# Fifth raw weight tile and two-part bias matmul in the first stage, two recurrence projections beside keys and values in the mixer

## The chip, the cores and the metric

The kernel runs on one core of a Trainium2 chip. The metric is the device time of one execution in microseconds, the median of three runs. TensorE (PE) does the matmuls, VectorE (DVE) and ScalarE (ACT) the elementwise work, GpSimd (POOL) small work and its own DMA queue, SyncE (SP) issues the weight DMAs.

## The reference

A hybrid encoder of two layers on a sequence of 256 positions and 1024 channels, in float32. Every layer is a half-weighted gated feed-forward block, a mixer, and a second feed-forward block, with a final norm behind the last layer:

```python
for l in range(DEPTH):                       # DEPTH = 2
    x = x + 0.5 * swiglu(rms_norm(x, ffn1_norm[l]), ffn1_w_gate[l], ffn1_w_up[l], ffn1_w_down[l])
    h = rms_norm(x, mix_norm[l])
    xr, gate, q, k, v = jnp.split(h @ w_in[l], SPLITS, axis=-1)   # 512, 512, 512, 128, 128 columns
    y_rec = recurrent_group(xr, gate, ...)   # convolution of 4 taps, two gated linear recurrences
    y_att = windowed_gqa(q, k, v, attn_sink[l], rel_bias)         # 8 heads, 2 key heads, window 128
    x = x + concat([rms_norm(y_rec, ...), rms_norm(y_att, ...)]) @ w_out[l]
    x = x + 0.5 * swiglu(rms_norm(x, ffn2_norm[l]), ...)
return rms_norm(x, final_norm)
```

The feed-forward width is 2816. The attention bias is a table of 32 rows per head, looked up by the bucket of the distance.

## The kernel before, in words

All products are of float32 accuracy, made of TensorE's faster format fp32r: a value is split into a high part (a rounding copy) and a low part (the value less the high part), and three products are summed. Weights come from DRAM as raw tiles of 1 MB (`load_raw`, L225 to L249, on SP's queue), a column chunk of 256 columns ("kc") or 256 rows ("rc"). There are RAWS = 3 raw buffers, and raw number 3 goes into another tile ("w") that is free until the first mixer. `prep_one` (L268 to L311) turns a raw tile into halves of 128x1024: ACT makes the high part (L303; for a few names DVE does, L301), DVE the low part (L304). Halves go into a ring of SLOTS = 8 slots; the two of the mixer's keys and values ("kv", 0 and 1) go into the tiles "w" and "i" in its stead. When the last half of a raw tile is made, the next raw tile is loaded into its buffer. Halves are made AHEAD = 3 places ahead of the matmul that uses them.

There are six stages: feed-forward, mixer, feed-forward, twice. PE, SP and POOL run in the order of the program text; on ACT and DVE a planner orders the work by what is ready and, among that, by the text, except in the first steps (FIRST, L53), the last and where a helper says so.

A feed-forward stage takes its 22 units of 128 columns in turn. Units 0 and 1 are done together, positions as stationary operand (`head`, L690, with 512 moving columns; in the first stage `first_head`). The others are done by `gu` (L749), weights as stationary operand: a product for the gate (g2, g3, ...), one for the up projection (u2, u3, ...), each some 2.8 us of PE, then `whole`, `gated` and `split_h` on ACT and DVE. `head_end` (L726) transposes units 0 and 1 behind u2 and splits them. Down products (d0, d1, ...) follow five units later. All gate and up products take their PSUM bank from two pools of two banks in turn (`bank("gc")`).

In the first stage the order of raw tiles is gate and up of units 0/1 (raw 0, 1), of units 2/3 (2, 3), of units 4/5 (4, 5), down of units 0/1 (6), gate of 6/7 (7), and so on. Raw 0 and 1 are split in quarters by `first_prep` (L251; token w11 is the high part of the second quarter of raw 1, on ACT). The stage also fetches parameters: `setup_params` at unit 4 (POOL's queue), the recurrence's gate weights (`load_gates`, L359, a memset and eight DMAs on POOL's queue into tile "i", at unit GLOAD = 4), the mixer's gain (`load_gain(1)`, L1149, SP's queue, before the unit loop) and, at unit 9, `setup_params2` with the bias product of the table (33x8) and a 33x512 one-hot (L458, plain float32).

At the boundary to a mixer (`boundary`, L588) the last down products run (`tail`), the rows are normalized, `transposes(0)` turns the first 128 positions, `head(0)` computes keys and values of these, `transposes(1)` and `head(1)` do the other 128. In the mixer `head` (L846) is 24 matmuls of 256 columns by `natural` (L545). Then the units follow in the list ORDER (L59): x is one of four recurrence inputs (`xr`, L868: 24 matmuls of 256 columns, then the convolution `conv`, L873, four DVE steps that read the PSUM bank), k turns the keys (`head_end`, L861), q queries, l the recurrence's gate products (`lru_gate`, L891: 12 matmuls into two banks, eight ACT steps), L attention logits (`att_logits`, L959: two banks, four DVE steps and four ACT exponentials), g the output gate, P, V, s, c, y, D, O, r, R, S the rest.

Of the kernel before, what the change touches and what calls it, by code (L numbers as in the profile page):

```python
# [8 lines left out]
F32 = mybir.dt.float32  # L9
F32R = mybir.dt.float32r  # L10
# [21 lines left out]
MIXF = 0  # L32
TAIL = 4
HB = 7
GLOAD = 4
GSPLIT = 12
X1 = False
EXTRA = {("kv", 0): "w", ("kv", 1): "i"}
# [17 lines left out]
CUT = 3  # L56
RCUT = 1
EARLY = 1
ORDER = "x0 k0 x1 q0 l0 q1 l1 L0 x2 L1 x3 g0 l2 P0 q2 l3 V0 P1 s0 L2 g1 c0 c1 q3 V1 P2 L3 c2 y0 g2 y1 V2 P3 g3 c3 V3 D0 y2 y3 r0 O0 r1 O1 r2 r3 R0 R1 R2 R3 S0".split()  # L59
HEAD = 2  # L60
VO = 6
VG = 1
# [5 lines left out]
def encoder_kernel(  # L68
# [81 lines left out]
    def cols(w, c):  # L150
        return add_raw(w[:, c:c + 256].rearrange("(k p) c -> p k c", p=128), "kc")
# [7 lines left out]
    def head_half(name, r, j):  # L159
        add_half(name, [(r, j)], "kh")  # L160
# [26 lines left out]
        down(NM // 2 - 1)  # L187

    def plan_mix(st, wi, wo):
        r = cols(wi, 1536)  # L190
        for j in range(2):
            head_half((st, "kv", j), r, j)
        chunk = {}

        def chunk_of(n, p):
            if (n, p) not in chunk:
                chunk[n, p] = cols(wi, {"x": 0, "g": 512, "q": 1024}[n] + p * 256)
            return chunk[n, p]

        for n, i in ORDER:  # L200
            i = int(i)
            if n in "xg":
                col_half((st, {"x": "xr", "g": "gt"}[n], i), chunk_of(n, i // 2), i % 2)
            elif n == "q":
                add_half((st, "q", i), [(chunk_of("q", h), i * 64, h * 64, 64) for h in range(2)], "kc")
        for p in range(4):
            r = rows(wo, p * 256)
            for j in range(2):
                add_half((st, "o", 2 * p + j), [(r, j)], "rc")
# [15 lines left out]
    def load_raw():  # L225
        r = state["raw"]
        if r >= len(raws):
            return
        src, shape = raws[r]
        if r == RAWS:  # L230
            t = w_p.tile([128, 2048], F32, tag="w", name="raw")
        else:
            t = raw_p.tile([128, 2048], F32, tag="raw", name="raw")
        if shape == "kc":
            v = t.rearrange("p (k c) -> p k c", k=KD)
        else:
            v = t.rearrange("p (k c) -> p k c", k=2)
        raw_t[r] = (v, src)
        if r < 2:
            if r == 1:  # L240
                for q in range(4):
                    if q == XQ:
                        load_x(1)
                    for n in range(2):
                        vv, ss = raw_t[n]
                        nc.sync.dma_start(out=vv[:, 2 * q:2 * q + 2, :], in_=ss[:, 2 * q:2 * q + 2, :])
        else:
            nc.sync.dma_start(out=v, in_=src)
        state["raw"] = r + 1  # L249

    def first_prep(lo, n, q):  # L251
        name = ((0, 0), "gu"[n], q // 2)
        if name not in slot_t:
            slot_t[name] = tuple(ring_p.tile([128, 1024], F32R, tag=w, name=w) for w in ("wh", "wl"))
        src = raw_t[n][0][:, 2 * q:2 * q + 2, :]
        c = q % 2 * 512
        h3, l3 = (w[:, c:c + 512].rearrange("p (k c) -> p k c", k=2) for w in slot_t[name])
        if lo:
            dve.tensor_sub(out=l3, in0=src, in1=h3.bitcast(F32))
        else:  # L260
            act.activation(out=h3, in_=src, func=AF.Copy)
        if lo and n and q == 3:
            state["half"] = 4
            for n in range(2):
                del raw_t[n]
                load_raw()

    def prep_one():  # L268
        j = state["half"]
        name, pieces, form = halves[j]  # L270
        for pc in pieces:
            while state["raw"] <= pc[0]:
                load_raw()
        if name in turns:
            wh = ring_p.tile([128, 1024], F32R, tag="wh", name="wh")
            wl = ring_p.tile([128, 1024], F32R, tag="wl", name="wl")
        else:
            n = EXTRA[name[1:]]
            if n == "pr":
                wh, wl = (pr_p.tile([128, 1024], F32R, tag=n, name="w_pr") for _ in range(2))  # L280
            else:
                w = {"w": w_p, "i": mix_p}[n].tile([128, 2048], F32R, tag=n, name="w_" + n)
                wh, wl = w[:, 0:1024], w[:, 1024:2048]
        for pc in pieces:
            v = raw_t[pc[0]][0]
            if form == "kc":
                _, c, d, n = pc
                src = v[:, :, c:c + n]
                h3 = wh.rearrange("p (k c) -> p k c", k=KD)[:, :, d:d + n]
                l3 = wl.rearrange("p (k c) -> p k c", k=KD)[:, :, d:d + n]  # L290
            elif form == "kh":
                src = v[:, 4 * pc[1]:4 * pc[1] + 4, :]
                h3, l3 = (w.rearrange("p (k c) -> p k c", k=4) for w in (wh, wl))
            elif form == "gu":
                src = v[:, 2 * pc[1]:2 * pc[1] + 2, :]
                h3, l3 = (w.rearrange("p (k n c) -> p k n c", k=2, n=2)[:, :, pc[2], :] for w in (wh, wl))
            else:
                src = v[:, pc[1], :]
                h3, l3 = wh, wl
            if name[0][1] == 1 and name[1:] in VHI:  # L300
                dve.tensor_copy(out=h3, in_=src)  # L301
            else:
                act.activation(out=h3, in_=src, func=AF.Copy)  # L303
            dve.tensor_sub(out=l3, in0=src, in1=h3.bitcast(F32))  # L304
        slot_t[name] = (wh, wl)
        state["half"] = j + 1
        for pc in pieces:
            if last_use[pc[0]] == j:
                del raw_t[pc[0]]
                if pc[0] != RAWS:  # L310
                    load_raw()  # L311

    def prefetch(target):
# [122 lines left out]
    def setup_params():  # L436
        tmp = a_p.tile([128, 2, 512], F32, tag="a", name="tmp")
        rows_t = tmp[:N_ROWS, 0, :]
        srcs = [(R_CONVW, conv_w.rearrange("l j c -> (l j) c")), (R_CONVB, conv_b),
                (R_BA, lru_b_a.rearrange("l d c -> (l d) c")), (R_BX, lru_b_x.rearrange("l d c -> (l d) c")),  # L440
                (R_LAM, lru_lambda.rearrange("l d c -> (l d) c")), (R_GREC, lru_out_norm), (R_GATT, attn_out_norm)]
        for r, s in srcs:
            pool.dma_start(out=rows_t[r:r + s.shape[0], :], in_=s)
        pool.dma_start(out=sink_t, in_=attn_sink.partition_broadcast(128))
        rb = mix_p.tile([128, T], F32, tag="k", name="rb")[:33, :NH]
        oh = tmp[:33, 1, :]
        pool.memset(rb[32:33, :], -1e30)
        pool.dma_start(out=rb[0:32, :], in_=rel_bias)
        pool.dma_start(out=oh, in_=onehot)
        return tmp, rows_t, rb, oh  # L450

    def setup_params2(tmp, rows_t, rb, oh):
        ps = bank("gc")
        for c in range(NT):
            pe.transpose(ps[:, c * N_ROWS:(c + 1) * N_ROWS], rows_t[:, c * 128:(c + 1) * 128], eye_t[:N_ROWS, :N_ROWS])
        act.activation(out=par.rearrange("p a b -> p (a b)"), in_=ps[:, :NT * N_ROWS], func=AF.Copy)
        ps = bank("gc")
        pe.matmul(ps[:NH, :], rb, oh, start=True, stop=True)  # L458
        line = tmp[:NH, 0, :]
        act.activation(out=line, in_=ps[:NH, :], func=AF.Copy)  # L460
        ld = dram.tile([NH, 512], F32, name="ld")
# [220 lines left out]
    def ffn(st, acc_done):  # L682
# [112 lines left out]
        def body():  # L795
            nd = 0
            for m in range(HEAD, NM):
# [6 lines left out]
                if m == HEAD:  # L804
                    head_end()
                if st == (0, 0):
                    if m == 4:
                        late_setup.append(setup_params())
                    if m == 9:
                        setup_params2(*late_setup.pop())  # L810
# [16 lines left out]

    def mix(l):
        st = (l, 1)
        ps_x = {}  # L830
        xch_t, xcl_t = {}, {}
        xc_t, ge_t, a_t, yh_t, yl_t = {}, {}, {}, {}, {}
        q_t = mix_p.tile([128, NT, T], F32R, tag="q", name="q_t")
# [10 lines left out]
            return ps  # L844

        def head(t):  # L846
            if t == 0:
                ps_x["kv"] = bank("gc")
            ps = ps_x["kv"]
            natural([ps[:, t * 256:t * 256 + 256]], [[W(st, "kv", j) for j in range(2)]], t)  # L850
            if t == 1:
                for j in range(2):
                    done((st, "kv", j))
                new_tiles()
                act.activation(out=kv_t.rearrange("p t c -> p (t c)"), in_=ps, func=AF.Copy)

        def new_tiles():
            late["w"] = w_p.tile([128, 2 * NT, T], F32, tag="w", name="w_t")
# [7 lines left out]
            dve.tensor_sub(out=kl_t, in0=ps[:, 0:T], in1=k_t.bitcast(F32))  # L866

        def xr(i):  # L868
            ps = unit("xr", i)
            with tc.high_priority(offset=MIXF):  # L870
                conv(i, ps)

# [258 lines left out]
    with tc.manual_schedule(engines={engines.PE, engines.SP, engines.Pool}):  # L1131
# [4 lines left out]
            step[n.upper()] = lambda *a, f=f: f(True, *a)  # L1136
        with tc.manual_schedule(engines={engines.Activation, engines.DVE}):
            setup_early()
            for _ in range(RAWS + 1):
                load_raw()  # L1140
            for tok in FIRST:
                ins = step[tok[0]](*map(int, tok[1:]))
                if tok in BEHIND:
                    state["behind"].append(ins)
# [1 line left out]
        state["behind"] = [ins]  # L1146
        prefetch(3 + LEAD2)
        state["behind"] = []
        load_gain(1)  # L1149
        for s in range(3 * DEPTH):  # L1150
            _, body, tail, evac = stages[s]
            body()
# [54 lines left out]
```

## Time and profile before

| | |
|---|---|
| median of 3 runs | 940.21 us (939.73 to 942.36) |
| the profiled execution, its own time | 940.3 us |
| its span in the trace | 938.5 us |
| PE busy | 925.9 us (99%) |
| DVE busy | 696.5 us (74%) |
| ACT busy | 544.7 us (58%) |
| POOL busy | 37.0 us (4%) |
| granted TensorE clock, mean | 0.999 |

Times in the trace count from the start of the span. The ends of matmuls are modelled, so that a matmul of 256 columns is shown with some 0.28 us although the next starts 0.12 us later: what a matmul costs is read from start to start.

### The profile page before, as it was taken

Reading aid. Unit: us, or ns where it says so; the run is one execution under the profiler, and the core shown is the slowest. Engines: PE = TensorE matmul, PEld = TensorE weight load, DVE = VectorE, ACT = ScalarE, POOL = GpSimd, SP = SyncE. Lnnn points to the kernel's source line nnn. Section 1 sums busy time; section 2 is a strip of 40 time slices with the busy share of each in tenths; the row PEclk is TensorE's granted clock in tenths of the full one; section 3 lists DMA queues with packets and bytes.
Section 4 is the critical chain, followed back from the end, with each engine's and each line's share of the span. In section 5 each row is a group of like instructions: output and inputs, shape, how many; then the busy total and the mean of one; then the engine's idle time right before and its main releaser. Section 6 shows DMA issues by size and latency. Waiting matters only on the chain.

```text
span 938.5 us, 13682 instructions
## 1 busy us (share of the span) xinstructions
PE 925.9 (99%) x5288; PEld 804.8 (86%) x5288; DVE 696.5 (74%) x1212; ACT 544.7 (58%) x1006; POOL 37.0 (4%) x58
## 2 busy tenths in 40 slices
PE   8999999999999999999999999999999999999997
PEld 7888888889988888888888888888999888888885
DVE  6877666759998866666688666666799887666663
ACT  7755555547865655555466555554687565555542
POOL 4100000000010000000030000000000100000000
PEclk9999999999999999999999999999999999999999
DMA  8966955614255866565557565655162566665521
GB/s 279 304 211 200 326 192 183 228 64 154 91 157 179 262 197 191 179 192 196 175 174 252 181 186 198 199 179 179 49 223 68 180 233 203 197 196 182 184 86 45
DMA packets 124993, 172.54 MB, mean 184 GB/s; under 512 B 3920, under 2 KB 108792, under 8 KB 124928
## 3 DMA queue, kind: packets, MB, share of 16 engines
q1 hardware_dynamic: 122192, 166.21, 54.7%
q0 software_dynamic: 2288, 4.87, 1.6%
q8 instruction: 41, 0.67, 0.3%
q10 hardware_dynamic: 448, 0.59, 0.2%
q14 instruction: 24, 0.20, 0.1%
HBM read 170.59 MB, written 3.16 MB: 185 GB/s over the span
## 4 chain that ended last, share of the span: by engine, by line
PE 92%; ACT 2%; DVE 2%; DMA 1%; issue 1%; POOL 0%; POOLq 0%; DVEq 0%; ACTq 0%
PE ps_g L572 16%; PE ps_c L572 15%; PE ps_g L571 7%; PE ps_c L571 7%; PE ps_a L581 5%; PE ps_a L583 4%; PE ps_a L582 4%; PE ps_b L582 4%; PE ps_b L583 4%; PE ps_b L581 4%; PE ps_g L697 2%; PE ps_c L697 2%; PE ps_a L1010 1%; PE ps_g L561 1%; PE ps_g L560 1%; PE ps_g L562 1%
## 5 line engine op out<-in xcount | busy, mean ns | idle before, releaser
L304 DVE TENSOR_TENSOR wl<-raw,wh 128x1024 fp32r<-128x1024 f32 (+1 forms) x320 | 367.4, 1157 | 106.3 <-ACT wh L303 101.9
L303 ACT ACTIVATE wh<-raw 128x1024 fp32r<-128x1024 f32 (+1 forms) x306 | 301.6, 1000 | 89.0 <-PE ps_b L583 61.8
L572 PE MATMUL ps_g<-xhl,wh 128*128 128x512 f32 x640 | 231.5, 396 | 1.5 <-DVE hl L746 1.5
L572 PE MATMUL ps_c<-xhl,wh 128*128 128x512 f32 x640 | 231.2, 396 | 0.0
L571 PE MATMUL ps_g<-xhl,wl 128*128 128x256 f32 x560 | 156.5, 279 | 0.0
L571 PE MATMUL ps_c<-xhl,wl 128*128 128x256 f32 x560 | 156.2, 279 | 0.0
L572 PEld LDWEIGHTS ps_g<-xhl,wh 128*128 128x128 f32 x640 | 120.3, 188 | 24.6 <-issue 1.7
L572 PEld LDWEIGHTS ps_c<-xhl,wh 128*128 128x128 f32 x640 | 120.2, 188 | 22.8
L571 PEld LDWEIGHTS ps_g<-xhl,wl 128*128 128x128 f32 x560 | 105.6, 189 | 3.5
L571 PEld LDWEIGHTS ps_c<-xhl,wl 128*128 128x128 f32 x560 | 105.5, 188 | 3.5
L581 PE MATMUL ps_a<-wh,hh 128*128 128x512 f32 x168 | 65.8, 392 | 0.0
L581 PE MATMUL ps_b<-wh,hh 128*128 128x512 f32 x168 | 65.7, 391 | 0.0
L583 PE MATMUL ps_b<-wh,hl 128*128 128x512 f32 x168 | 65.4, 389 | 0.0
L582 PE MATMUL ps_b<-wl,hh 128*128 128x512 f32 x168 | 65.4, 389 | 0.0
L583 PE MATMUL ps_a<-wh,hl 128*128 128x512 f32 x168 | 65.4, 389 | 0.0
L582 PE MATMUL ps_a<-wl,hh 128*128 128x512 f32 x168 | 65.4, 389 | 0.0
L757 ACT ACTIVATE sg<-ps_g 128x256 f32<-128x256 f32 x40 | 15.4, 385 | 63.5 <-PE ps_g L572 63.5
L757 ACT ACTIVATE sg<-ps_c 128x256 f32<-128x256 f32 x40 | 15.3, 383 | 55.3 <-PE ps_c L572 54.6
L758 DVE TENSOR_TENSOR sg<-ps_g,sg 128x256 f32<-128x256 f32 x40 | 17.0, 425 | 32.1 <-ACT sg L757 32.1
L757 ACT ACTIVATE su<-ps_c 128x256 f32<-128x256 f32 x40 | 15.3, 382 | 38.7 <-PE ps_c L572 38.7
L582 PEld LDWEIGHTS ps_a<-wl,hh 128*128 128x128 f32 x168 | 31.6, 188 | 6.9
L583 PEld LDWEIGHTS ps_a<-wh,hl 128*128 128x128 f32 x168 | 31.5, 188 | 6.9
(320 smaller groups left out, 1579.2 us busy)
## 6 DMA issues: line engine op xcount, KB each, us to landing
raw<-in_ffn_w_down_dram SPq DMA_DIRECT2D x44, 1024.0 KB, 5.0
raw<-in_ffn_w_gate_dram SPq DMA_DIRECT2D x43, 1024.0 KB, 5.4
raw<-in_ffn_w_up_dram SPq DMA_DIRECT2D x43, 1024.0 KB, 5.4
raw<-in_w_in_dram SPq DMA_DIRECT2D x14, 1024.0 KB, 5.4
raw<-in_w_out_dram SPq DMA_DIRECT2D x8, 1024.0 KB, 7.3
lb<-ld POOLq DMA_DIRECT2D x1, 2048.0 KB, 14.8
bias_t<-lb POOLq DMA_DIRECT2D x1, 1536.0 KB, 12.5
gain<-in_ffn_norm_dram SPq DMA_DIRECT2D x3, 512.0 KB, 4.3
```

The costliest lines, as they stand in the source:

```text
L303: act.activation(out=h3, in_=src, func=AF.Copy)
L304: dve.tensor_sub(out=l3, in0=src, in1=h3.bitcast(F32))
L560: pe.matmul(dst, wh[:, ks], xh[:, k, t0:t1], start=(k == 0), stop=False)
L561: pe.matmul(dst, wh[:, ks], xl[:, k, t0:t1], start=False, stop=False)
L571: pe.matmul(dst[:, 0:T], wl[:, ks], x2[:, 0, k, :], start=False, stop=False)
L572: pe.matmul(dst, wh[:, ks], x2[:, :, k, :], start=(k == 0), stop=(k == KD - 1))
L581: pe.matmul(acc[hf], ah[:, ts_], wh[:, cs], start=first, stop=False)
L582: pe.matmul(acc[hf], ah[:, ts_], wl[:, cs], start=False, stop=False)
L583: pe.matmul(acc[hf], al[:, ts_], wh[:, cs], start=False, stop=last)
L697: pe.matmul(ps, x, w[k // 2][p % 2][:, k % 2 * 512:k % 2 * 512 + 512], start=(p == 0 and k == 0), stop=(p == 2 and k == KD - 1))
L757: act.activation(out=s, in_=ps[:, T:2 * T], func=AF.Copy)
L758: dve.tensor_tensor(out=s, in0=ps[:, 0:T], in1=s, op=ALU.add)
```

## The change

1. A fifth raw tile: raw number 4 goes into the tile "i" and is loaded at the start, behind raw 3. So raw 5 and 6 go into the buffers of raw 0 and 1, and so on, one further for each.
2. GLOAD goes from 4 to 7 for both layers, and `load_gain(1)` from before the unit loop to unit 8.
3. The high part of token w11 is made by DVE and not by ACT.
4. The bias product: POOL splits the table in a high and a low part (two instructions), the one-hot is loaded into the tile "ql", and two fp32r matmuls take the place of the float32 one.
5. In both mixers, columns 0 to 255 of the input projection (recurrence inputs 0 and 1) are computed in `head` with keys and values: four halves "kv" of the form "gu" (512 columns: 256 of keys and values, 256 of the recurrence), 24 matmuls of 512 columns for each 128 positions. ACT copies both parts out of PSUM for each 128 positions. `xr(0)` and `xr(1)` become two transposes each into one shared bank; the convolution reads that bank. The halves of x0 and x1 go.
6. ORDER: `x0 k0 x1 q0 l0 q1 l1 L0 x2 L1 x3 ...` becomes `q0 x0 k0 x1 q1 x2 l0 L0 l1 L1 x3 ...`, and the halves are planned in that order.

```diff
-GLOAD = 4
+GLOAD = 7
-ORDER = "x0 k0 x1 q0 l0 q1 l1 L0 x2 L1 x3 g0 l2 P0 q2 l3 ...
+ORDER = "q0 x0 k0 x1 q1 x2 l0 L0 l1 L1 x3 g0 l2 P0 q2 l3 ...
     def plan_mix(st, wi, wo):
-        r = cols(wi, 1536)
-        for j in range(2):
-            head_half((st, "kv", j), r, j)
-        chunk = {}
+        chunk = {("x", 0): None}
+        r = cols(wi, 1536), cols(wi, 0)
+        for q in range(4):
+            add_half((st, "kv", q), [(r[0], q, 0), (r[1], q, 1)], "gu")
...
             t = w_p.tile([128, 2048], F32, tag="w", name="raw")
+        elif r == RAWS + 1:
+            t = mix_p.tile([128, 2048], F32, tag="i", name="raw")
...
             dve.tensor_sub(out=l3, in0=src, in1=h3.bitcast(F32))
+        elif (n, q) == (1, 1):
+            dve.tensor_copy(out=h3, in_=src)
...
-                if pc[0] != RAWS:
+                if pc[0] not in (RAWS, RAWS + 1):
                     load_raw()
...
-        oh = tmp[:33, 1, :]
+        once = mix_p.tile([128, NT, T], F32R, tag="ql", name="once")
+        oh = once[:33, 0:2, :].rearrange("p a b -> p (a b)")
+        rbs = [once[:33, 2, 8 * n:8 * n + NH] for n in range(2)]
...
+        pool.tensor_copy(out=rbs[0], in_=rb)
+        pool.tensor_tensor(out=rbs[1], in0=rb, in1=rbs[0].bitcast(F32), op=ALU.subtract)
...
-        pe.matmul(ps[:NH, :], rb, oh, start=True, stop=True)
+        for n in range(2):
+            pe.matmul(ps[:NH, :], rbs[n], oh, start=(n == 0), stop=(n == 1))
...
+                    if m == 8:
+                        load_gain(1)
...
         def head(t):
-            if t == 0:
-                ps_x["kv"] = bank("gc")
-            ps = ps_x["kv"]
-            natural([ps[:, t * 256:t * 256 + 256]], [[W(st, "kv", j) for j in range(2)]], t)
+            ps = bank("gc")
+            ts_ = slice(t * 128, (t + 1) * 128)
+            w = [W(st, "kv", q) for q in range(4)]
+            for p in range(3):
+                for k in range(KD):
+                    x = cur["l" if p == 2 else "h"][:, k, ts_]
+                    pe.matmul(ps, x, w[k // 2][p % 2][:, k % 2 * 512:k % 2 * 512 + 512],
+                              start=(p == 0 and k == 0), stop=(p == 2 and k == KD - 1))
+            act.activation(out=kv_t[:, t, :], in_=ps[:, 0:T], func=AF.Copy)
+            xn_x[t] = sum_p.tile([128, T], F32, tag=("sg", "su")[t], name="xn_x")
+            act.activation(out=xn_x[t], in_=ps[:, T:2 * T], func=AF.Copy)
...
         def xr(i):
-            ps = unit("xr", i)
+            if i < 2:
+                if i == 0:
+                    ps_x["x"] = bank("gc")
+                ps = ps_x["x"][:, i * T:(i + 1) * T]
+                for t in range(2):
+                    pe.transpose(ps[:, t * 128:(t + 1) * 128], xn_x[t][:, i * 128:(i + 1) * 128], eye_t)
+            else:
+                ps = unit("xr", i)
...
-            for _ in range(RAWS + 1):
+            for _ in range(RAWS + 2):
                 load_raw()
...
-        load_gain(1)
```

## Rows read from the trace of the kernel before

**Rows 1.** The page: busy time, share of the span and instructions of an engine.
```profile
PE 925.9 (99%) x5288; PEld 804.8 (86%) x5288; DVE 696.5 (74%) x1212; ACT 544.7 (58%) x1006; POOL 37.0 (4%) x58
```

**Rows 2.** Waits of PE, two of them: us in total, times, longest.
```profile
PE ps_g L572 <- DVE hl L746: 1.5, 1, 1.5
...
PE ps_b L535 <- DVE xn L517: 0.9, 2, 0.4
```

**Rows 3.** Timeline of PE, 37.2 to 39.9 us: start, us, instruction, idle before and releaser.
```profile
37.58 0.40 PE L572 MATMUL ps_c<-xhl,wh 128*128 128x512 f32 x1
39.44 0.47 PE L572 MATMUL ps_g<-xhl,wh 128*128 128x512 f32 x1 [1.46 <-DVE hl L746]
```

**Rows 4.** The chain that ended last, 17 to 40 us: start, us, what.
```profile
25.94 8.10 DMA raw<-in_ffn_w_down_dram
...
38.88 0.43 DVE hl L746
```

**Rows 5.** Timeline of DVE between 24 and 37 us.
```profile
35.21 1.23 DVE L304 TENSOR_TENSOR wl<-raw,wh 128x1024 fp32r<-128x1024 f32 x1 [2.34 <-ACT wh L303]
```

**Rows 6.** Timeline of SP, 0 to 60 us: DMAs issued.
```profile
19.12 0.39 SPq L248 DMA_DIRECT2D raw<-in_ffn_w_up_dram  x1
25.94 0.37 SPq L248 DMA_DIRECT2D raw<-in_ffn_w_down_dram  x1
26.35 0.47 SPq L354 DMA_DIRECT2D gain<-in_mix_norm_dram  x1
```

**Rows 7.** Timeline of POOL, 12 to 100 us: the gate weights' memset.
```profile
19.74 1.82 POOL L361 MEMSET gw<- 128x2048 f32 x1
```

**Rows 8.** Stretches of the first stage: busy us of PE, PEld, DVE, ACT, POOL; clock, DMA share, GB/s.
```profile
16.00:24.00 8.00, 8.00 (x66) 7.96 (x67) 6.94 (x17) 6.52 (x12) 6.46 (x11) 1.00 0.87 252
...
32.00:40.00 8.00, 6.54 (x39) 5.49 (x38) 5.37 (x11) 5.33 (x10) 0.00 (x0) 1.00 1.00 330
```

**Rows 9.** Timeline of PE, 81 to 83.2 us: the bias product.
```profile
81.62 1.02 PE L458 MATMUL ps_g<-tmp,rb 33*8 33x512 f32 x2
82.57 0.51 PE L581 MATMUL ps_a<-wh,hh 128*128 128x512 f32 x1
```

**Rows 10.** Timeline of the start, 0 to 40 us: the second norm's first step.
```profile
12.08 0.21 DVE L497 TENSOR_SCALAR rstd<-ss 128x1 f32<-128x1 f32 x1 [0.45 <-ACT ps_b L407]
```

**Rows 11.** Timeline of PE, 196 to 240 us, at the first mixer.
```profile
199.72 0.64 PE L552 MATMUL ps_c<-w_w,xhl 128*128 128x256 f32 x4
...
203.13 1.54 PE L535 MATMUL ps_b<-eye_t,xn 128*128 128x128 f32 x8 [0.44 <-DVE xn L517]
...
213.61 0.28 PE L560 MATMUL ps_c<-xhl,wh 128*128 128x256 f32 x1
```

**Rows 12.** Timeline of PE, 286 to 302 us, at the boundary to the next feed-forward stage.
```profile
286.65 1.03 PE L535 MATMUL ps_a<-eye_t,xn 128*128 128x128 f32 x8
287.44 0.48 PE L581 MATMUL ps_b<-wh,yh 128*128 128x512 f32 x1
...
288.21 1.98 PE L697 MATMUL ps_c<-wh,xhl 128*128 128x512 f32 x8
...
300.31 0.39 PE L572 MATMUL ps_c<-xhl,wh 128*128 128x512 f32 x1
```

**Rows 13.** Timeline of DVE, 210.4 to 217.7 us: the first convolution.
```profile
210.72 0.54 DVE L877 TENSOR_SCALAR xc<-ps_g,par 128x256 f32<-128x256 f32 x1 [2.95 <-PE ps_g L562]
...
212.72 0.48 DVE L880 SCALAR_TENSOR_TENSOR xc<-ps_g,par,xc 128x255 f32<-128x255 f32 x1
```

**Rows 14.** A stretch of the first mixer, columns as in rows 8.
```profile
230.00:270.00 40.00, 39.96 (x324) 38.00 (x324) 39.05 (x96) 32.29 (x83) 2.29 (x2) 1.00 0.30 96
```

**Rows 15.** Timeline of SP, 183 to 187 us.
```profile
185.32 0.37 SPq L248 DMA_DIRECT2D raw<-in_w_in_dram  x1
```

**Rows 16.** Waits between 195 and 235 us: a wait of PE's weight loads.
```profile
PEld ps_c L560 <- DVE xc L880: 0.2, 1, 0.2
```

**Rows 17.** Timeline of ACT, 222.9 to 228.3 us: a step of the recurrence's gates.
```profile
222.96 0.47 ACT L908 ACTIVATE w_t<-ps_g,hba 128x256 f32<-128x256 f32 x1
```

## Prediction before the result

> **What bounds the kernel now.** The page first: PE is busy 99% of the span, DVE 74%, ACT 58% [rows 1]. So only two things can be gained: matmul time itself, and the few places where PE stands still. Next the waits of PE: its longest is 1.5 us, once, on the low part of a split, and one of 0.4 stands there twice, on the norm [rows 2]. The timeline shows where: the product u4 of the first stage starts at 39.44, although its predecessor started at 37.58 and a matmul of 512 columns takes some 0.23 from start to start [rows 12], so 39.44 - 37.81 = 1.63 us are lost [rows 3]. The chain of waits tells why: it goes back through DVE's split (38.88) to the DMA of the first down tile, raw 6, issued at 25.94 and under way for 8.10 us [rows 4]. ACT, in its planned order, stood in front of that tile; behind it on ACT stood the copies that free the PSUM bank u4 wants, and DVE waited 2.34 us for ACT, until 35.21 [rows 5]. The other stops are at the two mixers' boundaries, where PE waits for the norm of the second 128 positions [rows 2, 11], once in each mixer. All else is matmul time.
>
> **First stage, the raw tiles.** Raw 6 was issued at 25.94 because its buffer was raw 2's. Now it takes raw 1's and goes out where raw 5 did, at 19.12 [rows 6], 6.8 us sooner. It will not land 6.8 us sooner, since the DMA engines are full: 330 GB/s at share 1.00 [rows 8]. Ahead of it in the old order lay 0.5 MB of gate weights (POOL, from 19.74 [rows 7]) and beside it 0.5 MB of gain (26.35 [rows 6]): both go behind. The gate weights now wait for raw 4's last reader in tile "i", which ends near 27 us, POOL being otherwise free to run ahead of PE; the gain waits on SP behind the raw tiles that precede unit 8. Between 16 and 24 us the DMA engines had a share of 0.87 [rows 8], the pause that the earlier raw 4 fills, another 0.6 MB. Of some 1.1 MB removed or filled, at 330 GB/s, come 3.4 us: raw 6 lands near 30.7, at most 1 us either way, where it landed at 34.1. The bank of u4 has to come free 1.6 us sooner, so a landing up to 32.5 is enough. I take the whole 1.63 us; bounds 0 (another wait ends last) and 1.63. What is late next? DVE is the engine to watch: of the eight microseconds from 32 it is busy 5.37 [rows 8], and nearly all the rest is that one wait. But it gains these 2.34 us [rows 5], more than PE gains, so it stays ahead. The gate weights' splits (eight instructions) come later than before, off this stretch.
>
> **Start.** Token w11's copy leaves ACT. The second norm waited 0.45 us on ACT behind the squares [rows 10]; now DVE carries the copy, in its own order ahead of that norm: some 0.4 us, an estimate from a split of 1024 columns at 1.23 [rows 5], of which it has half the columns and one operand less. Of the pause 0.1 is left as gain, bounds 0 and 0.45. The fifth load is issued behind all quarters of raw 0 and 1 on the same queue, so it delays none of them: nothing.
>
> **Bias product.** From 81.62 to 82.57 the float32 matmul, two instructions, holds PE for 0.95 us [rows 9]. Two fp32r matmuls of 512 columns take 0.23 each from start to start [rows 12], 0.46: gain 0.48, bounds 0.3 and 0.5. POOL's two small instructions wait for the table's DMA, and behind them on POOL stand only the gate weights, which wait anyway; PE needs them 50 us later: nothing.
>
> **Mixer, the boundary.** From the first matmul of `head(0)` to the end of x1, PE takes 213.61 - 199.72 = 13.89 us, with the wait for the second norm in it [rows 11]. The new order has the same form as a feed-forward boundary: 24 matmuls of 512 columns, eight transposes, 24 more, 300.31 - 288.21 = 12.10 us [rows 12]; less the transposes' 0.79 that is 0.236 for a matmul, almost without a wait, because the longer `head(0)` covers the norm. Added are the transposes of x0, x1 and, as before, k0: eight take 287.44 - 286.65 = 0.79 [rows 12] when they stand alone, so six take 0.6. Together 12.7 and some 0.1 for turning from transposes to matmuls: 12.8, a gain of 1.1 us for each mixer. In streaming alone nothing is gained, since a matmul of 512 columns costs just what two of 256 do; the 1.1 is the wait. ACT has two more copies of 256 columns for each 128 positions, covered by q0's 2.9 us (24 matmuls of 256 columns at 0.12), which now stands between `head(1)` and x0.
>
> The Trainium skill (TensorE: Matmul & The Clock Gate, Part 4: PE-mode transpose) speaks against this part: it gives some 275 ns for a 128x128 transpose inside a kernel. By that the four added ones would cost 1.1 us and not 0.4, and the sum would be 1.4 us higher over both mixers; the trace has 0.79 us for eight [rows 12], so the row decides.
>
> **Mixer, the new order.** x0's convolution starts behind q0 and the transposes, near 199.7 + 12.1 + 2.9 + 0.3 = 215.0, where it started at 210.72 [rows 13], and l0 and l1 have only L0 between them, no longer a projection of 2.9 us. Banks decide, four in turn by two pools. Counting requests, the second bank of L0 is x2's: x2's convolution must have read it. That takes 213.20 - 210.72 less a foreign step of 0.42, some 2.1 us [rows 13], and between x2 and that matmul lie l0 (12 matmuls) and three of L0, 15 x 0.12 = 1.8 us, while the hand-over from PE to DVE costs 0.2 more: a stop of 0.5, up to 1.7 if DVE has just begun a weight split of 1.23 [rows 5], none if the planner puts the bank's choice otherwise. x3 takes l1's first bank, which ACT frees after l0's eight steps of some 0.47 [rows 17]: 0 if these come right behind the matmuls, 2.0 if L0's exponentials go ahead of them; I take 0.3, since those exponentials first need four DVE steps. Against that, the old stop of 0.2 before g0, where x2's convolution was late, goes [rows 16]. For each mixer 1.1 + 0.2 - 0.8 = 0.5 us gained; bounds +1.3 and, with 1.7 and 2.0 of stops, -2.4.
>
> **The sum.** 1.63 + 0.1 + 0.48 + 2 x 0.5 = 3.2 us off the profiled execution's 940.3 (its span 938.5 and 1.8 around it), which lies 0.1 above the median: 937.1.
>
> **The rivals.** (A) No new stop in the mixers, 1.3 us gained in each: 940.3 - 2.2 - 2.6 = 935.5. For it: before, PE had only one stop of 0.2 in a mixer's body. Against: banks follow closer on each other now. (B) The stop in the first stage only changes its cause: the gate weights fall into the loads of raw 7 and 8, or DVE's order puts the down tile's split ahead of `head_end`'s; 937.1 + 1.6 = 938.7. For it: DMA and DVE are both full there. Against: the margin between a landing at 30.7 and one at 32.5. (C) The mixers give back what they save: stops of 1.3 to 2.5 us in each, 938.1 to 940.5. (D) Slower: DVE is the second bound of the mixer, 39.05 of 40 us between 230 and 270 [rows 14]. The convolutions start 4.3 us later; what DVE can't fill with weight splits until then is lost to it. If all of it is lost, less the 0.95 us that it has idle there, the end of each mixer moves 3.3 us out: 940.3 - 2.2 + 6.6 = 944.7; with half of it lost, 940.5. It decides once over 1 us of DVE work is pushed into that stretch; against it, the halves of g0 and q2 (3 us of DVE) are free to fill the pause. That the weights of the longer head come late is no rival of weight: all four halves need both raw tiles, but the last was split by 185.3, when the next load could go out [rows 15], and the head starts at 199.72.
>
> The Trainium skill (the same page, Back-to-back issue gap) names 131 ns for each matmul of 512 columns in a sustained stream: by that the 48 of a mixer's two heads would save another 4.6 us and each mixer with it, 927.9 in all. The trace has at most 0.236 us for each of 48 [rows 12] and no row near 131: I give it one chance in a hundred, within (A).
>
> **Chances.** The forecast 0.40 (936.2 to 938.0), A 0.20, B 0.20, C 0.14, D 0.06. A measurement of this kernel tells about 0.3% from no change, that is 2.8 us: faster means under 937.4. A, three quarters of the forecast's case and a little of B fall there, 0.55; nearly all of D gives 0.05 for slower; 0.40 remain for no difference. The range leaves out A's lower edge and D: 934.8 to 939.9.
>
> **What the changed profile would show.** Right: no wait of PE near 38 us, and raw 6 issued near 19 us and landed before 32.5; two L-lines of fp32r bias matmuls within 0.5 us; PE from `head(0)` to `head(1)`'s end without a wait of over 0.3 us, some 12 us; small stops at L0 and x3. Wrong: a stop of over 1 us between 35 and 60 us (B), PE waiting on `conv` or on ACT's gate steps for over 1.3 us in a mixer (C), or DVE idle before 215 and PE waiting on DVE behind 230 (D).

## The result and the profile after

The changed kernel takes 950.77 us (median; 949.98 to 953.9), the kernel before beside it 940.22 (939.73 to 942.36): ratio 1.0116, interval 1.0101 to 1.0132. It is slower by some 10.5 us; forecast was 937.1, with a range of 934.8 to 939.9. The profiled execution took 950.95 us, its span 949.2.

The page of after and its waits of PE, against [rows 1, 2]: busy time, share and instructions of an engine; then us in total, times, longest.

```profile
PE 928.6 (98%) x5200; PEld 802.6 (85%) x5200; DVE 697.3 (73%) x1221; ACT 545.3 (57%) x1019; POOL 37.4 (4%) x60
...
PE ps_g L893 <- DVE xc L906: 6.8, 2, 3.4
PE ps_c L991 <- DVE stm L1000: 1.6, 2, 0.8
...
PE ps_c L993 <- DVE ql_t L1131: 0.8, 2, 0.4
```

The two waits that were to go are gone: the 1.5 us on the down tile's split, and the 0.9 on the second norm. In their place stand waits inside the mixers, twice each, once for each of the two mixers. The largest is 3.4 us: the transposes of x1 (L893) wait until the convolution of x0 (L906) has read.

The first stage came close to the forecast. PE's timeline of after at the place of [rows 3], SP's at that of [rows 6], and the bias product, against [rows 9]:

```profile
37.52 0.40 PE L583 MATMUL ps_c<-xhl,wh 128*128 128x512 f32 x1
37.75 0.39 PE L583 MATMUL ps_g<-xhl,wh 128*128 128x512 f32 x1
...
18.29 0.37 SPq L252 DMA_DIRECT2D raw<-in_ffn_w_up_dram  x1
18.89 0.39 SPq L252 DMA_DIRECT2D raw<-in_ffn_w_down_dram  x1
...
79.89 0.63 PE L469 MATMUL ps_g<-once 33*8 33x512 f32 x2
80.45 0.50 PE L592 MATMUL ps_a<-wh,hh 128*128 128x512 f32 x1
```

The down tile is read from 18.89 on (25.94 before), and ScalarE's first copy of it starts at 28.78 (34.12 before); u4 follows 0.23 us behind its predecessor, and the bias product holds PE for 0.56 us instead of 0.95. To see where time is won or lost, the starts of the same down products (the stream's lines) were subtracted, after less before: -1.73 us near 64 us, -2.17 from 91 to 198; then +4.75 behind the first mixer and, almost unchanged up to the second, +10.65 behind that. So 2.17 us are won and 6.9 and 5.9 lost, in the mixers but for 0.3 in the transposes right behind the second (from 755.77 on).

The first mixer of after, timeline of PE, against [rows 11]:

```profile
197.56 0.63 PE L866 MATMUL ps_c<-w_w,xhl 128*128 128x512 f32 x2
...
203.14 1.04 PE L546 MATMUL ps_b<-eye_t,xn 128*128 128x128 f32 x8
...
209.99 0.28 PE L571 MATMUL ps_c<-xhl,wh 128*128 128x256 f32 x1
...
212.87 0.38 PE L893 MATMUL ps_g<-eye_t,xn_x 128*128 128x128 f32 x2
213.08 0.38 PE L883 MATMUL ps_c<-eye_t,kv_t 128*128 128x128 f32 x2
...
216.85 0.69 PE L893 MATMUL ps_g<-eye_t,xn_x 128*128 128x128 f32 x2 [3.39 <-DVE xc L906]
217.19 0.56 PE L571 MATMUL ps_g<-xhl,wh 128*128 128x256 f32 x1
217.55 0.41 PE L572 MATMUL ps_g<-xhl,wh 128*128 128x256 f32 x1
217.76 0.41 PE L573 MATMUL ps_g<-xhl,wl 128*128 128x256 f32 x1
...
226.57 0.38 PE L991 MATMUL ps_c<-k_t,q_t 64*128 64x256 f32 x1 [0.20 <-DVE xc L906]
...
230.54 0.38 PE L991 MATMUL ps_c<-k_t,q_t 64*128 64x256 f32 x1 [0.82 <-DVE stm L1000]
```

And VectorE there, against [rows 13] (columns as there):

```profile
212.67 0.69 DVE L307 CAST wh<-raw 128x1024 fp32r<-128x1024 f32 x1 [5.38 <-DMA raw<-in_w_in_dram]
213.29 0.54 DVE L903 TENSOR_SCALAR xc<-ps_g,par 128x256 f32<-128x256 f32 x1
...
214.08 0.47 DVE L905 SCALAR_TENSOR_TENSOR xc<-ps_g,par,xc 128x254 f32<-128x254 f32 x1
...
214.80 0.47 DVE L905 SCALAR_TENSOR_TENSOR xc<-ps_g,par,xc 128x255 f32<-128x255 f32 x1
215.19 1.21 DVE L310 TENSOR_TENSOR wl<-raw,wh 128x1024 fp32r<-128x1024 f32 x1
216.32 0.47 DVE L906 SCALAR_TENSOR_TENSOR xc<-ps_g,par,xc 128x255 f32<-128x255 f32 x1
```

x0's convolution starts at 213.29 (210.72 before, when the first stage ended 2.17 us later), and until 212.67 VectorE has stood for 5.38 us: next in its order is g0's cast, whose weights are still being read. Then a split of 1.21 us falls between the convolution's third and fourth step. Both parts of x lie in one bank, x1's transposes wait for the last reader of x0's part, and with them all that follows on PE. A ledger of the first mixer: `head(0)` to q0's start takes 209.99 - 197.56 = 12.43 us, where it took 13.89 to x1's end before [rows 11]: 1.5 won. Lost are the transposes' own 0.55, the stop of 3.55 between starts (213.08 to 216.85 less 0.22), 1.3 in q1, whose first products follow each other 0.21 us apart instead of 0.12, and stops of 0.36, 0.99, 0.30, 0.58 and 0.42 up to 258 us: 8.0. Less the 1.5 that is 6.5 of the measured 6.9.

### The profile page after: what moved, and what is told of

Read it like the earlier page. It is cut to its first block, busy times and chain, and to the rows that moved or that the text cites. A ratio compares the mean times of both kernels' runs of the same rounds, so it can differ in the third digit from the quotient of the medians.

```text
span 949.2 us, 13525 instructions
## 1 busy us (share of the span) xinstructions
PE 928.6 (98%) x5200; PEld 802.6 (85%) x5200; DVE 697.3 (73%) x1221; ACT 545.3 (57%) x1019; POOL 37.4 (4%) x60
## 4 chain that ended last, share of the span: by engine, by line
PE 91%; DVE 4%; ACT 2%; DMA 1%; issue 1%; POOL 0%; POOLq 0%; DVEq 0%
PE ps_g L583 16%; PE ps_c L583 16%; PE ps_g L582 7%; PE ps_c L582 7%; PE ps_a L592 4%; PE ps_a L594 4%; PE ps_b L593 4%; PE ps_b L594 4%; PE ps_b L592 4%; PE ps_a L593 4%; PE ps_g L708 2%; PE ps_c L708 2%; PE ps_c L866 1%; DMA raw<-in_w_in_dram 1%; PE ps_a L1036 1%; PE ps_c L585 1%
## 5 line engine op out<-in xcount | busy, mean ns | idle before, releaser
L756 ACT ACTIVATE hh<-th 128x256 fp32r<-128x256 f32 x80 | 33.3, 417 | 8.4 <-DVE th L750 8.1
```

What stands on the lines that cost most here:

```text
L756: act.activation(out=hh, in_=src, func=AF.Copy)
```

## Experiments

All times are medians; the kernel before stood at 940.07 to 940.32 in these runs.

**Only the first stage.** e3_first_stage: after, with the mixer (plan, head, order) of before.

```diff
 # from after, shortened
-ORDER = "q0 x0 k0 x1 q1 x2 l0 L0 l1 L1 x3 ...   # and head, plan_mix, xr
+ORDER = "x0 k0 x1 q0 l0 q1 l1 L0 x2 L1 x3 ...   # as before
```

> The first-stage parts alone (fifth raw tile, later gate weights and gain, w11 on DVE, two-part bias product); mixer and its order as in the kernel before. Both theories: 940.2 - 2.2 = 938.0, since the trace of the changed kernel is 2.16 us ahead at the last down products of the first stage. If the mixer at its old order were upset by the earlier start, it would be above 939.

Measured: 938.16, ratio 0.9981 (0.9972 to 0.9990). The gain holds by itself (1.9 us by medians), and this form is a little faster than the kernel before. So the change is two: one that wins 2 us and one that loses 12.6. In e3 the first convolution starts as soon as x0's product ends:

```profile
208.52 0.54 DVE L888 TENSOR_SCALAR xc<-ps_g,par 128x256 f32<-128x256 f32 x1 [2.95 <-PE ps_g L571]
```

**The shared bank.** e1_four_at_once puts the four transposes of x0 and x1 ahead of the first convolution; e2_own_bank gives x1 a bank of its own.

```diff
 # e1, at x0
+for c in range(2):
+    for t in range(2):
+        pe.transpose(ps_x["x"][:, c * T + t * 128:...], xn_x[t][:, c * 128:...], eye_t)
 # e2
-ps = ps_x["x"][:, i * T:(i + 1) * T]
+ps = bank("gc")[:, 0:T]
```

> The changed kernel, but the transposes of x0 and x1 (four) all stand ahead of x0's convolution; one bank as before. Theory 'bank': x1's transposes wrote the bank that x0's convolution was still reading, and PE stood 3.55 us for it in each mixer, after which the first mixer ran twelve matmuls at half the clock (1.1 us more). Without that wait 950.8 - 2 x 3.55 - 1.1 = 942.6, if the later stops at L0, L1 and x3 (some 2.7 us in each mixer) stay as they are. Rival 'order': DVE is simply behind, since the convolutions start late and l0 and l1 follow each other closely; then PE reaches l0 and L0 3.6 us sooner and waits there for the convolution of x1 and x2 instead, giving back 2 us or more in each mixer: 946.5 or above.

> The changed kernel, but x1 gets a PSUM bank of its own; the transposes stay where they were (x0, k0, x1). Theory 'bank': the wait of 3.5 us at x1's transposes is gone as with four transposes at once, about 942.6; the request for one more bank shifts the later ones by one, so the stops at L0 and x3 may change place by up to 1 us in each mixer. If the wait stays with a bank of its own, the cause is not the shared bank but the order of DVE.

Measured: 952.42 and 949.88, against 950.77. The wait at x1 is gone in both and the time hardly moves. Waits of PE in e1_four_at_once, and a stretch of each of its mixers (columns as in [rows 8]):

```profile
PE ps_c L928 <- DVE xc L908: 3.6, 2, 2.1
PE ps_c L993 <- ACT i_t L937: 2.2, 2, 1.1
```

```profile
208.00:240.00 32.00, 29.06 (x200) 27.10 (x199) 24.95 (x59) 20.08 (x51) 0.00 (x0) 0.84 0.48 165
672.00:704.00 32.00, 28.58 (x201) 26.61 (x200) 25.48 (x59) 19.41 (x49) 0.00 (x0) 0.89 0.47 163
```

The gates (L928) now wait for the convolutions, the logits (L993) for ScalarE's gate steps. But the time alone would mislead here, because TensorE's granted clock was lower too: 0.84 and 0.89 in these stretches, 0.95 and 1.00 in the same ones of after. What is missing to full clock is at most 32 x 0.16 + 32 x 0.11 = 8.6 us in e1 and 32 x 0.05 = 1.6 in after. So up to 7 us of e1's time are the clock's, and they hide what the lost wait gave back. The fairer view is e2's first mixer, where the clock stood at 1.00: from `head(0)` to the transposes behind the mixer it takes 91.83 us, after's 93.83 and e3's 86.93. With a bank of its own 4.9 of the 6.9 us lost are still there. The shared bank is where most of the delay showed, not what made it.

**Order or head.** e4_old_order is e1 with the old order; e6_order_alone is e3 with the new order and x0, x1 as products of their own.

```diff
 # e4 (from e1)
-"q0 x0 k0 x1 q1 x2 l0 L0 l1 L1 x3 ..."
+"x0 k0 x1 q0 l0 q1 l1 L0 x2 L1 x3 ..."
 # e6 (from e3): the reverse
```

> The changed kernel with four transposes at once and with the old order (x0 k0 x1 q0 l0 q1 l1 L0 x2 L1 x3). Theory 'bank': the order of units matters little once the wait is gone, 942 to 943, less what the wider spacing of l0 and l1 gives. Rival 'order': the convolutions start 2.9 us earlier, behind a stop of 0.9 us for the copy of head(1)'s last bank, and l0 and l1 are apart again: the stops at L0, L1 and x3 go, 938 to 940.

> The first-stage parts and the mixer before, with only the changed kernel's order of steps (q0 first, x2 ahead of l0, l1 behind L0); x0 and x1 stay products of their own. With the runs so far it fills a table of two by two: products or one head with transposes, old order or new. Theory 'the products were the cover': with them in place the convolutions still have PE work beside them and the order costs little, 938 to 940. Theory 'the order costs by itself' (the old order with the head was 944.9, the new one with the head and all four transposes at once 952.4): 943 to 946.

Measured: 944.89 and 944.45. With 938.16 (neither) and 952.42 (both) that is a table of two by two: the order costs 6.3 or 7.5 us, the head 6.7 or 8.0. Either alone makes the kernel slower. In e3, e4 and e6 the clock stood at 1.00 in both stretches (208 to 240, 672 to 704). Only e1's was lower, and at full clock e1 would lie, by the estimate above, somewhere between 943.8 and 952.4. So the two costs of the step alone are shown, but not that they add up. Waits of PE in e4, then in e6:

```profile
PE ps_g L928 <- ACT xch L916: 2.8, 2, 1.4
PE ps_c L893 <- ACT xn_x L870: 1.3, 2, 0.6
```

```profile
PE ps_c L976 <- ACT i_t L920: 2.7, 2, 1.4
```

With the head, x0's convolution starts at 211.21 (its transposes wait 0.6 us for ScalarE's copy of x) and the gates wait for it; in e3 it starts at 208.52, and nothing waits. With the order, l0 is followed at once by L0: each takes both banks, and L0 waits 1.4 us until ScalarE has read l0's.

**Is VectorE blocked?** Its 5.38 us before the first convolution suggest so. e5_swap_g0_q2 exchanges g0 and q2 in the order, and with them their splits; e7_g0_no_wait takes g0's weights from a chunk that is already there (half of the gate is then made of other weights).

```diff
 # e5
-... x3 g0 l2 P0 q2 l3 ...
+... x3 q2 l2 P0 g0 l3 ...
 # e7
-chunk_of(n, i // 2)
+chunk_of("x" if n + str(i) == "g0" else n, 1 if n + str(i) == "g0" else i // 2)
```

> The changed kernel with the places of g0 and q2 exchanged in the mixer's order (and so in the order in which their weights are split); nothing else. In the changed kernel VectorE stands 5.38 us in order on g0's weights (still being read) while q2's weights are already there, and q2's two low parts (0.68 us each) then fall between the steps of the convolutions. Theory 'VectorE is blocked in order': q2's parts go into the pause, each mixer gets some 1.2 to 2 us back, 947.0 to 948.5. Theory 'late products': the convolutions cannot begin before 213 us whatever VectorE did before, and the stops are the products' that used to lie beside them: 950 to 951.

> The changed kernel, with g0's weights cut from the chunk that x2 and x3 use, which is already there, so that VectorE's cast of g0 waits for no read (the first half of the gate's weights is thereby another one; the count of splits, products and elementwise steps is the same, one read of 1 MB comes later). Theory 'VectorE is blocked in order': g0's 1.9 us and q2's 1.36 us of VectorE go into the pause of 5.4 us, the two convolutions end up to 3.3 us earlier, 944 to 947. Theory 'late products': the convolutions start at 213.3 us as before and x1's transposes still wait for the first of them; 949 to 951.

Measured: 959.03 and 957.04, slower than after by 8 and 6 us, and outside both expectations: the theory falls, and the rival didn't foresee a loss either. Timeline of VectorE in e7_g0_no_wait:

```profile
207.19 0.69 DVE L307 CAST wh<-raw 128x1024 fp32r<-128x1024 f32 x1
207.92 2.43 DVE L310 TENSOR_TENSOR wl<-raw,wh 128x1024 fp32r<-128x1024 f32 x3
213.24 0.54 DVE L903 TENSOR_SCALAR xc<-ps_g,par 128x256 f32<-128x256 f32 x1 [2.90 <-PE ps_g L893]
...
215.62 1.22 DVE L310 TENSOR_TENSOR wl<-raw,wh 128x1024 fp32r<-128x1024 f32 x1 [0.39 <-ACT wh L309]
216.76 0.47 DVE L906 SCALAR_TENSOR_TENSOR xc<-ps_g,par,xc 128x255 f32<-128x255 f32 x1
```

The pause is filled, and the convolution starts at 213.24, as in after: what it waits for is PE's transposes. Then the next split stands between its steps, and waits itself for ScalarE; x1's transposes wait 3.9 us. The clock was lower too, 0.92 from 208 to 250 us and 0.89 from 672 to 704: at most 42 x 0.08 + 32 x 0.11 = 6.9 us, against 1.6 in after, so up to 5 of the 6 us more can be the clock's. That filling the pause gains nothing rests on the convolution's start, not on the time.

**More products in between.** e8_more_cover moves x3 ahead of the gates in e1; e11_between puts a product between each two steps that take both banks; e10_q0_first_only is e3 with only q0 moved to the front.

```diff
 # e8:  q0 x0 k0 x1 q1 x2 x3 l0 L0 l1 L1 g0
 # e11: q0 x0 k0 x1 q1 l0 x2 L0 l1 x3 L1 g0
 # e10: q0 x0 k0 x1 l0 q1 l1 L0 x2 L1 x3 g0   (products, old head)
```

> The form with all four transposes at once (952.4) with x3's product moved ahead of the first gates, so that 2.9 us more of products that need no convolution lie between the transposes and the gates. Theory 'lost cover': most of that 2.9 us fills the stops at L0 and l1 (1.24 + 0.37 and 1.75 us in each mixer) and the clock is not halved behind them: 946 to 949. Theory 'VectorE's work sets the end of the stretch': x3's convolution joins VectorE's queue earlier and the stops move on, 951 to 954.

> The form with the head and all four transposes at once (952.4), its order changed to q0 x0 k0 x1 q1 l0 x2 L0 l1 x3 L1 g0: a product between each pair of steps that take both banks. Theory 'two banks': the stops at L0 (1.24 + 0.37 us) and at l1 (1.75 us) go, and the halved clock from 224 to 232 us with them: 944 to 947.5, less what l0 waits for the first convolution. Rival 'VectorE's chain is late wherever the products stand': 950 or more.

> First-stage parts and the old mixer with x0 and x1 as products; of the new order only q0's move to the front (q0 x0 k0 x1 l0 q1 l1 L0 x2 L1 x3), so that products still lie between gates and logits. The whole new order cost 6.3 us here (944.45 against 938.16), with a stop of 1.52 us in each mixer where the first logits wait for ScalarE to read the first gates' bank. Theory 'two banks': the cost comes from l0 L0 l1 L1 in a row, each of which takes both banks; with q1 back between them 938 to 940, unless l0 now waits for the first convolution (then up to 942). Rival 'q0 first': 943 to 945.

Measured: 953.46, 953.37 and 946.35. No place for the products helps (e8's clock was still lower than e1's, a mean of 0.987 against 0.990). q0 at the front alone costs 8 us, more than the whole new order (up to 1.6 of them are the clock's, 0.95 from 672 to 704). Waits of PE in e10:

```profile
PE ps_g L911 <- ACT xch L899: 3.0, 2, 1.6
```

So "two banks" is not the whole cause: once q0 stands in front, the first gates are too early for the convolution, which starts at 211.44 instead of 208.52.

**Splits between the steps.** e9_conv_first (from after) and e12_head_conv_first (from e4) queue the later splits behind the second convolution.

```diff
 # shortened
+state["cap"] = index[st, "xr", 3]        # until x1
 # at x1
+state["cap"] = 1 << 30
+state["behind"] = [late["conv"]]         # the second convolution's last step
```

> The changed kernel, with g0's, q2's and the later weights split behind the second convolution on VectorE's queue (no split between the steps of the two convolutions); the work is the same. In the changed kernel the first convolution takes 3.4 us (213.29 to 216.7) of which 1.21 us are a split, the second 4.0 us (217.65 to 221.7) of which 3.2 us are splits. Theory 'splits between the steps': x1's transposes wait some 1.4 us less, the second convolution ends 3 to 4 us earlier, the stops behind it (0.36, 0.99, 0.30 us) shrink; 944.5 to 947.5. Rival 'backlog': the 4 to 5 us of splits are owed all the same and come out behind the gates and logits; 949.5 to 953.

> The form with the head, all four transposes at once and the old order (944.89), with the later weights split behind the second convolution. There the first gates waited 1.57 + 0.55 us for the first convolution, between whose steps lie 1.9 us of splits. Theory 'splits between the steps': the stop goes nearly whole, 940.5 to 942.5. Rival 'backlog': 944 to 947. Below 938.2 (the best form so far, products as before) the head would be worth having; by its stops alone (0.8 us at the transposes, 0.3 at the boundary, 1 us later in each mixer) it should stay above that.

Measured: 949.47 (1.3 us less) and 943.95 (0.9 less): nearer the rival. For e12 that is clear, since neither e4 nor e12 had a lower clock in its mixers. For e9 it is less so: its clock was 0.95 in both stretches, in after in the first alone, which is up to 1.6 us. In e9 the second convolution ends 3.2 us earlier, yet:

```profile
PE ps_g L893 <- DVE xc L906: 4.8, 2, 2.4
PE ps_c L991 <- ACT i_t L935: 2.7, 2, 1.4
```

One stop shrinks by 1.0 us and another grows at the logits, as in e6.

**The chain or the sum.** Two theories were left: VectorE's whole work between 208 and 260 us sets the end, or the length of the first chain does (transposes, two convolutions, gates, logits). e13_fewer_taps_01 and e14_fewer_taps_23 take the same four VectorE steps out of after, inside the first convolutions and behind the first gates; e15_old_fewer_taps and e16_old_more_taps take eight steps from, and add eight to, the old mixer.

```diff
-for j, d, n in ((0, 2, T - 2), (1, 1, T - 1)):
+for j, d, n in ((0, 2, T - 2), (1, 1, T - 1)) if c in (2, 3) else ():   # e13; e14: (0, 1)
+for j, d, n in ((0, 2, T - 2), (1, 1, T - 1)) if c in () else ():       # e15, from e3
+for j, d, n in ((0, 2, T - 2), (1, 1, T - 1)) * 2:                      # e16, from e3
```

> The changed kernel with two of the four taps left out of the convolutions of parts 0 and 1 (four VectorE steps of 0.4 us fewer in each mixer, all on the way to x1's transposes and the first gates). Theory 'VectorE's sum': 1.6 us in each mixer, 947.5 (947 to 948.3). Theory 'length of the first chain': the wait of x1's transposes loses the 0.8 us of part 0 and what stood between its steps (1.2 us), and the second convolution ends 1.6 to 3 us earlier: 943 to 946.5.

> The changed kernel with two of the four taps left out of the convolutions of parts 2 and 3 (the same four VectorE steps fewer in each mixer, but behind the first gates). Theory 'VectorE's sum': as much as with parts 0 and 1, 947.5 (947 to 948.3). Theory 'length of the first chain': next to nothing, 949.8 to 950.8.

> First-stage parts with the old mixer (938.16), two of four taps left out of all four convolutions: eight VectorE steps, 3.2 us, fewer in each mixer. TensorE has no stop of over 0.3 us in that mixer's body, so if TensorE's sum is its bound, nothing is gained: 937.6 to 938.3. If VectorE's sum is the bound there too: 932 to 935.5.

> First-stage parts with the old mixer, two of the taps done twice in all four convolutions: eight VectorE steps, 3.2 us, more in each mixer. VectorE is idle for 1.6 us there between 208 and 260 us. Theory 'VectorE is the close second bound': the time grows by 3.2 less 1.6 us in each mixer, 941.4 (940.5 to 944.6). Theory 'slack elsewhere' (its splits for the later steps can move behind 260, where VectorE has some 10 to 20 per cent free): under 1 us in all, 938.2 to 939.2.

Measured: e13 946.38, 4.4 us less than after; e14 953.94 (951.3 to 956.84), not less; e15 939.1, e16 952.31. e14's profiled execution had after's clock (0.997) and after's time (951.3 against 950.95). Less work on VectorE helps only inside the first chain. Waits of PE in e13, e14, e16, then a stretch of e13 and one of e16's second mixer:

```profile
PE ps_g L893 <- DVE xc L906: 2.4, 2, 1.3
PE ps_c L991 <- DVE xc L906: 1.8, 2, 0.9
```

```profile
PE ps_g L893 <- DVE xc L906: 6.8, 2, 3.4
PE ps_c L993 <- DVE ql_t L1131: 2.0, 2, 1.0
```

```profile
PE ps_c L911 <- ACT xch L899: 4.8, 4, 1.6
PE ps_c L978 <- DVE ql_t L1116: 1.8, 2, 0.9
PE ps_c L569 <- DVE stm L985: 1.4, 2, 0.7
```

```profile
216.00:220.00 4.00, 4.00 (x35) 4.00 (x34) 3.73 (x8) 1.20 (x3) 0.00 (x0) 1.00 0.00 0
...
708.00:714.00 6.00, 6.00 (x30) 5.67 (x31) 3.48 (x5) 3.79 (x10) 0.00 (x0) 0.50 0.12 50
```

In e13 x1's wait falls from 3.4 to 1.3, in e14 it is the same to the tenth. From `head(0)` to the transposes behind it, e13's second mixer takes 91.05 us and after's 92.53: 1.5 won for the 1.6 taken out, at full clock in both. The first takes 90.95 against 93.83, 2.9 won: there after's clock fell (0.57 from 216 to 220, see the last section) and e13's did not. So the 4.4 us are the 3.2 of the steps and the clock.

The old mixer gains nothing from a shorter chain (e15 is 0.9 us above e3), so there PE sets the end. But its slack is small: 0.8 us more in each of four convolutions, 3.2 us in each mixer, cost 14 us in all (e16), far outside both expectations. Its first mixer takes 93.05 us where e3's takes 86.93, at full clock; in the second the clock fell to its lower level, 1.2 GHz, from 708 to 714. e16 adds to the chain and to VectorE's sum alike, so it doesn't tell which of the two overflowed. The reading that the old mixer stood near an edge, and that the change pushed it over, fits e13 to e16; it was not tested further.

## Why the prediction was wrong

- **First stage, bias, start: right.** Forecast 1.63 + 0.1 + 0.48 = 2.2; the down products stand 1.73 us earlier near 64 us and 2.17 from 91 on, and e3 stands 1.9 us below the kernel before beside it (940.07 less 938.16). The mechanism is the forecast one: the down tile read from 18.89, no wait near 38 us. Of the terms the stop at u4 gave its 1.63 and the bias product 0.39 instead of 0.48. The tile came 2 us sooner than forecast (28.78 against 30.7), and the gate weights went out at 33.42, not near 27.
- **Mixer, the boundary: nearly right in its own time, wrong in what it left out.** 12.43 us to q0, 0.55 for x's transposes and some 0.2 for k0's give 13.2; 12.8 was forecast, with k0's in it. The matmuls of 512 columns kept their 0.23 us (24 from 197.56 to 203.14). For the transposes the row was the right price: one is shown with 0.27 us (median of 40 in after), but eight in a run start 0.11 apart. What failed is the reading of [rows 11]: the products of x0 and x1 were counted as PE time that moves into the head at no cost. They were also what lay beside the first convolution: before, x0's product ended and x1's 2.9 us ran while VectorE worked. Now x1's transposes stand there, and the next product behind them. e4 shows the price of that step alone, 6.7 us over both mixers, where 2.2 were to be won.
- **Mixer, the new order: wrong, with a price as high (6.3 us in e6).** The steps looked for were those that ask for a new bank; x1's transposes write into the half of a bank whose other half is still being read, and were missed: 3.4 us in each mixer. But e2 shows that finding it would have given the place and less than a third of the loss. The stops were sized one by one with each operation next to its need, 0.8 us in all; some 6 came in each mixer. The first convolution's start was forecast 4.3 us later and came 4.8 later (213.29 against 208.52 in e3), so the delay was known; what was not asked is whether the rest of the chain, to the gates and logits, has that much to spare. e10 tells that q0's 2.9 us alone are too much. For a mixer, 0.5 us won was forecast, and 6.9 and 5.9 were lost.
- **The clock was no term of the sum.** It fell behind the stop in the first mixer, some 1.3 us (see the last section).
- **Rival D had the sign and part of the mechanism** ("DVE idle before 215 and PE waiting on DVE behind 230", both seen), and was given 0.06. Its counter-argument failed: g0's and q2's halves were not free to fill the pause, as g0's weights were on their way until 212.67. Its price, 3.3 us in each mixer by VectorE's sum, was too small, and its form was wrong: e14 shows that the sum isn't what decides, and e7 that filling the pause gains nothing.
- **Against C:** stops of 1.3 to 2.5 us were its bounds; the sum of stops in a mixer was over 6.
- **A slip in the working:** at 0.236 us a matmul, the further 4.6 us for each mixer that got one chance in a hundred within A would be 5.0. Nothing else hangs on it.

What stays open: why the old mixer loses 6.1 us in e16's first mixer, at full clock, for 3.2 us of added steps. The traces show that splits and copies come to stand elsewhere in VectorE's and ScalarE's order each time (e7, e9, e14); that this makes the rest was not tested by itself. Nor does any run take work from ScalarE, for which the gates or logits wait in e6, e9 and e10. In e13 nothing is left over: the steps and the clock give its gain.

## What to carry to other kernels

When a product is merged into an earlier one, ask what ran beside it: its engine time is kept, its cover is lost, and the chain that starts behind it starts later. Look first for the slack of that chain (lengthen it a little and time it) and only then for single waits; a wait that is removed without that can come back at the next step, as in e1. Read the granted clock beside every time: in e1 up to 7 us more than in after were the clock's, and the times alone would have said that the lost wait was worth nothing. And split a change into its independent parts: here one part was worth 2 us and hid behind another that cost 12.

## Hardware that was not expected

After x1's stop TensorE's granted clock fell in one mixer and not in the other. Stretches of after, columns us, then busy us of PE, PEld, DVE, ACT, POOL; clock, DMA share, GB/s:

```profile
216.00:220.00 4.00, 3.15 (x15) 3.15 (x16) 4.00 (x8) 0.64 (x2) 0.00 (x0) 0.57 0.00 0
```

```profile
676.00:682.00 6.00, 3.13 (x27) 2.89 (x25) 3.61 (x7) 4.21 (x9) 0.00 (x0) 1.00 0.29 100
682.00:690.00 8.00, 7.44 (x62) 7.42 (x62) 7.82 (x17) 1.72 (x5) 0.00 (x0) 1.00 0.34 102
```

The stops were alike (3.55 us from 213.08, 3.59 behind 678.7). The clock of 0.57 is a mean of the two levels, 1.2 and 2.4 GHz, and q1's products 0.21 us apart instead of 0.12 show the lower one. q1 takes 4.15 us there and 2.95 in the second mixer, and x1's transposes 0.34 and 0.19: some 1.3 us, about what the first mixer lost more than the second (6.9 against 5.6 without the transposes behind it). In e7_g0_no_wait, with stops of 4.03 and 4.10 us, it fell in both:

```profile
218.00:224.00 6.00, 6.00 (x42) 6.00 (x42) 3.62 (x8) 2.13 (x4) 0.00 (x0) 0.78 1.00 346
...
682.00:688.00 6.00, 2.06 (x14) 1.82 (x13) 5.00 (x11) 3.28 (x6) 0.00 (x0) 0.73 0.28 77
```

Why it stayed at full speed after one stop of 3.59 us no run here tells.
